# Hawk/FoX decoder step: the second tile's high halves of keys and queries come by an on-chip copy instead of a second load

## The chip, the core and the metric

The kernel runs on one core of one Trainium2 chip. A core has a matrix engine (TensorE, "PE" in the profile, with its weight loads as "PEld"), VectorE (DVE), ScalarE (ACT), GpSimd (POOL) and SyncE (SP), which here does nothing but issue transfers. 16 DMA engines move data between HBM and the on-chip memory, whose tiles have up to 128 partitions (rows). The engines run their own instruction streams in order and wait for one another by semaphores. The metric is the device time of one execution in microseconds.

## The reference, cut to what matters

One step of a small hybrid decoder: a recurrent (RG-LRU) layer, then an attention layer with a forget gate. It runs on a new prompt of 2048 tokens and, beside it, on 8 sequences of 8 new tokens with a paged cache of 4096 past tokens each. The change touches the attention of the prompt alone:

```python
D_MODEL = 1024; SEQ = 2048; N_HEADS = 16; HEAD_DIM = 64
...
def fox_block(q, k, v, cq, ck, q_pos, k_pos):
    s = jnp.einsum('bqhd,bkhd->bhqk', q, k).astype(jnp.float32) * (HEAD_DIM ** -0.5)
    s = s + jnp.swapaxes(cq, 1, 2)[:, :, :, None] - jnp.swapaxes(ck, 1, 2)[:, :, None, :]
    mask = k_pos[None, :] <= q_pos[:, None]
    s = jnp.where(mask[None, None], s, -jnp.inf)
    p = jax.nn.softmax(s, axis=-1)
    return jnp.einsum('bhqk,bkhd->bqhd', p.astype(v.dtype), v)
...
def fox_mixer(x, k, v, cq, ck, q_pos, k_pos, w_in, w_out):
    ...
    return (o * jax.nn.silu(g)) @ w_out
```

`cq` and `ck` are running sums of the log forget values. All data is float32.

## The kernel before, in words

TensorE multiplies in a reduced float32 format, so the kernel keeps float32 accuracy by splitting numbers: x = high + low, and a product is high·high + high·low + low·high. Keys and queries of the prompt are written to HBM in both halves, features first: `kd` and `qd` are [1024 features, 2 halves, 2048 tokens]. In `kd` half 0 is the low part and half 1 the high part; in `qd` it is the other way round.

The execution has three large stages. First come the recurrent layer and the projections, then, from about 1750 us on, the prompt's attention with the decode of the 8 sequences interleaved, and last the output projection. The change lies in the attention.

The attention (`attention`) goes through 16 heads; a head is 40 steps, called ticks. A unit is a head and a block of 512 queries (`qc`, 0 to 3); a tick takes one unit and one block of 128 keys, so unit `qc` has 4(qc+1) ticks. Even heads take the units in the order 0, 1, 2, 3, odd heads in the order 3, 2, 1, 0. In a tick TensorE makes the scores `st` with two matmuls. L1592 multiplies `ka` and `qa`, which have 128 rows each: the low and high rows of the keys against the high and low rows of the queries, that is, both cross products at once. L1593 multiplies `kbt` and `qbt`: 64 rows of high halves, and below them rows for the forget sums, the ones and the row maxima. ACT takes the exponential into a buffer `p` (L1601; six buffers `p`, five `acc`), after every four ticks TensorE multiplies the four `p` with the values `vvt` (L1612), and POOL adds the four `p` into `acc` (recorded at the helper's L108). A `p` is free again when both have read it. At least 8 and up to 18 ticks ahead, another pass (`top`, L1431) multiplies the high halves alone, and DVE takes the row maxima (L1433, L1435).

How the tiles are loaded: `load_keys(h+1)` runs in the first tick of head h and loads 64 rows of high keys into one of two fixed tiles `kbt` (L1399) and three rows of sums (L1400). `load_head(h+1)` runs at tick 16 of head h and loads `ka`, 128 rows with low and high rows interleaved (L1406, two buffers), and the values (L1407). `load_unit` loads the high queries into one of six fixed tiles `qbt` (L1413), `load_low` all 128 rows of `qa` (L1419, four buffers). So the high halves are fetched from HBM twice. All these are issued by SP, except the first ones, before the first tick, which ACT issues; those of head 0 are cut in two by columns.

The order around it: `later` is a list of functions that are called a given number of ticks on. The decode of the cache is a generator that is advanced in proportion (`Side.along`); its page loads `raw` (L1093) are issued by SP in the same queue, and its matmuls (L1148, L1262) are pinned between the attention's. Loads under `paged()` stand behind the last page load. Apart from such pins, the instruction order of each engine is set when the program is built, by a scheduler with a timeline of its own.

Of the kernel before, what the change touches and what calls it, by code (L numbers as in the profile page):

```python
# [12 lines left out]
F32R = mybir.dt.float32r  # L13
# [7 lines left out]
P = 128  # L21
D = 1024
KB = 8
SEQ = 2048
# [4 lines left out]
HD = 64  # L29
# [29 lines left out]
OG = 1  # L59
NQ = 6  # L60
AFT = 14


class Turns:
# [17 lines left out]
def f(ap):  # L82

    return ap.bitcast(F32)
# [3 lines left out]
def tile_hawk_fox(  # L88
# [8 lines left out]
    V, A, G, T, S = nc.vector, nc.scalar, nc.gpsimd, nc.tensor, nc.sync  # L97
# [19 lines left out]
    def paged():  # L117

        return tc.issue_after(place["S"]) if "S" in place else ExitStack()
# [49 lines left out]
    def dt_(name, shape):  # L169
        return dram.tile(shape, F32, name=name, tag=name)  # L170
# [9 lines left out]
    kd_d, qd_d = dt_("kd", [D, 2, SEQ]), dt_("qd", [D, 2, SEQ])  # L180
# [41 lines left out]
    def sbuf(es, name, side=None):  # L222
        return es.enter_context(tc.tile_pool(name=name, bufs=1, side=side, reuse_waits="tile"))
# [150 lines left out]
    later = Later()  # L374
# [959 lines left out]
    def attention(es):  # L1334
        pool = sbuf(es, "att")
# [11 lines left out]
        kbs = [pool.tile([P, SEQ], F32R, name="kbt0")]  # L1347
        qbs = [pool.tile([P, 512], F32R, name=f"qbt{i}") for i in range(NQ)]
        maskb = pool.tile([P, 512], F32, name="maskb")
        kbs.append(pool.tile([P, SEQ], F32R, name="kbt1"))  # L1350
        for i in range(NQ):
            if i % 3 == 0 and i < 6:
                kb = kbs[i // 3]
# [30 lines left out]
        heads, qas, mxs, oTs_, sgt = {}, {}, {}, {}, {}  # L1384
# [4 lines left out]
        def halves(h):  # L1389
            return ((0, half), (half, SEQ)) if h == 0 else ((0, SEQ),)  # L1390


        queue = [A]

        def load_keys(h):
            kb = kbs[h % 2]
            loaded.add(h)
            for lo, hi in halves(h):
                queue[0].dma_start(f(kb[0:64, lo:hi]), kd_d[h * HD:(h + 1) * HD, 1, lo:hi])  # L1399
                queue[0].dma_start(f(kb[64:67, lo:hi]), nc_d[h, :, lo:hi])  # L1400

        def load_head(h):
            hr = slice(h * HD, (h + 1) * HD)
            ka = pool.tile([P, SEQ], F32R, name="ka", tag="ka", bufs=2)
            for lo, hi in halves(h):
                queue[0].dma_start(f(ka[:, lo:hi]), kd_d[h * HD:(h + 1) * HD, :, lo:hi].rearrange("d x t -> (d x) t"))  # L1406
            queue[0].dma_start(vvs[h % 2][:, :, :], v_d[:, hr].rearrange("(k p) d -> p k d", p=P))  # L1407
            heads[h] = ka

        def load_unit(u):  # L1410
            h, qc = units[u]
# [3 lines left out]
        def load_low(u):  # L1415
            if u < len(units):
                h, qc = units[u]
                qa = qas[u] = pool.tile([P, 512], F32R, name="qa", tag="qa", bufs=4)
                queue[0].dma_start(f(qa[:, :]), qd_d[h * HD:(h + 1) * HD, :, qc * 512:(qc + 1) * 512].rearrange("d x t -> (d x) t"))  # L1419

        def top(u, j, ck):

# [69 lines left out]
        def norm(pr, sums, q0, n, oT):  # L1492
# [10 lines left out]
            def gate(qc, sg):  # L1503
# [9 lines left out]
                if n == 4:  # L1513
                    later.after(AFT, store)
                else:
                    store()

            def fetch(qc):
                sg = pool.tile([P, 512], F32, name="sgt", tag="sgt", bufs=2)
                with paged():  # L1520
                    S.dma_start(sg[:, :], sg_d[pr * P:(pr + 1) * P, qc * 512:(qc + 1) * 512])
                later.after(3, lambda: gate(qc, sg))

            for qc in range(q0, q0 + n):
                later.after((3 + 2 * (qc % 2) + (AFT + 7) * (qc // 2) if n == 4 else 2 * (qc - q0)), lambda qc=qc: fetch(qc))

        tasks = [(u, j, ck) for u, (h, qc) in enumerate(units) for j in range(4) for ck in range(qc + 1)]
        nks = [(qc + 1) * 4 for _, qc in units]
        start = [sum(nks[:u]) for u in range(len(units))]
        done = [0, 0, 0]  # L1530

        def advance(tick):
# [6 lines left out]
            while done[0] < min(need, len(tasks)):  # L1539
# [5 lines left out]
                done[0] += 1  # L1545

        load_keys(0)
        tick = 0
        advance(-1)
        load_head(0)  # L1550
        load_low(0)
        load_low(1)
        queue[0] = S
        for _ in range(3):
# [11 lines left out]
                    return psum["dec"].tile([P, 512], F32, name="st", tag="do"[wide[0] // 2 % 2], bufs=1)  # L1566
            return ps3.tile([P, 512], F32, name="st", tag="st", bufs=2)

        lows = [2]

        def loads():
            while lows[0] < len(units):
                v = lows[0]
                if tick < (start[v - 2] if v < 4 else min(max(start[v - 2], start[v - 3] + AFT), start[v] - 3)):
                    break
                with paged():
                    load_low(v)
                lows[0] += 1
            h, k = divmod(tick, 40)
            if k == 16 and h + 1 < H:  # L1580
                with paged():
                    load_head(h + 1)

        for u, (h, qc) in enumerate(units):
            for k in range(nks[u]):
                loads()
                ka, kb = heads[h], kbs[h % 2]
                qa, qb = qas[u], qbs[u % NQ]
                lo = max(0, k - qc * 4) * P
# [41 lines left out]
                if k + sum(nks[u - u % 4:u]) == 0 and h + 1 < H:  # L1631
                    load_keys(h + 1)
# [156 lines left out]
    done = 9  # L1789
# [6 lines left out]
    done = max(done, 41)  # L1796
# [61 lines left out]
    psum["att"] = banks(att, "psa", 6)  # L1858
    cost = sum(4.1 * 0.42 * (512 - max(0, k - qc * 4) * P) + 213 for qc in range(4) for k in range(4 * qc + 4)) * H
    side.along(attention(att), ((16 - FIRST) * TURN - side.spent) / (cost * SPAN))  # L1860
    place.clear()
    side.upto(1e12)
# [38 lines left out]
```

## Time and profile before

| | |
|---|---|
| time, median of 3 runs | 3023.98 us (3017.05 to 3034.43) |
| the profiled execution | 3028.43 us, span 3026.4 us |
| TensorE clock granted, mean | 0.969 |
| HBM traffic | 514.22 MB read, 135.16 MB written |
| DMA queue of SP and ACT | 644.26 MB, 67.4% of 16 engines' span |

An engine's share of the span is the time in which it ran instructions. The "idle before" of a group of instructions names what released it: a wait. The profile's chain follows the last instruction back through what each step waited for. A row of a stretch gives, for a window in microseconds: its length, busy time of PE, PEld, DVE, ACT and POOL with the number of instructions, the granted clock, the mean busy share of the DMA engines and the rate in GB/s. A row of waits gives the total, the number and the longest.

### The profile page before, as it was taken

How to read it: one execution, taken by the hardware profiler on the slowest of the kernel's cores; microseconds unless marked ns; L12 is line 12 of the kernel's file. 1: busy time of each engine (PE TensorE's matmuls, PEld its weight loads, DVE VectorE, ACT ScalarE, POOL GpSimd, SP SyncE). 2: the span in 40 equal slices, each digit the busy share in tenths (PEclk: the TensorE clock that was granted, in tenths of full speed). 3: DMA queues.
4: the chain of work that ended last, by engine and by line, in shares of the span. 5: the costliest groups of instructions: out<-in, count | busy, mean ns of one | idle time of the engine just before them, and what ended most of it. 6: DMA issues, size and time to landing. Idle time of an engine off the chain costs nothing.

```text
span 3026.4 us, 60467 instructions
## 1 busy us (share of the span) xinstructions
PE 2803.4 (93%) x21614; PEld 2252.1 (74%) x21614; DVE 1805.5 (60%) x4012; ACT 1269.9 (42%) x2874; POOL 1084.4 (36%) x1199
## 2 busy tenths in 40 slices
PE   6998999998997999999999699998998999999998
PEld 5997789988887997888889556665665666565687
DVE  6877455425427775676564466656776756655344
ACT  4665342222125665534333234444544444355321
POOL 1653201000002653100000245665575656659422
PEclk9999999999998999999999889999999999999999
DMA  4224546888863226699999968898899888874343
GB/s 123 79 88 133 171 126 191 256 263 281 278 216 91 89 88 194 209 313 338 332 346 326 279 209 243 248 282 255 250 291 287 267 251 265 260 247 122 98 145 110
DMA packets 479103, 653.79 MB, mean 216 GB/s; under 512 B 91291, under 2 KB 277020, under 8 KB 471525
## 3 DMA queue, kind: packets, MB, share of 16 engines
q1 hardware_dynamic: 475174, 644.26, 67.4%
q10 hardware_dynamic: 3340, 3.56, 0.4%
q8 instruction: 171, 2.80, 0.4%
q0 software_dynamic: 288, 2.10, 0.2%
q14 instruction: 130, 1.06, 0.1%
HBM read 514.22 MB, written 135.16 MB: 215 GB/s over the span
## 4 chain that ended last, share of the span: by engine, by line
PE 59%; DMA 16%; DVE 9%; ACT 6%; SPq 5%; issue 3%; POOL 1%; ACTq 0%; DVEq 0%; POOLq 0%
PE ops L1612 7%; PE st L1592 4%; PE y L383 4%; PE y L384 4%; PE y L385 4%; DMA raw<-in_cache_k_dram 4%; PE sx L1431 4%; PE dO L1262 3%; DMA raw<-in_cache_v_dram 3%; PE st L1593 3%; PE dS L1148 3%; PE kv L383 3%; PE kv L385 3%; PE kv L384 3%; SPq L1093 2%
## 5 line engine op out<-in xcount | busy, mean ns | idle before, releaser
L108 POOL TENSOR_TENSOR acc<-acc,p 128x512 f32<-128x512 f32 (+3 forms) x576 | 640.9, 1114 | 347.7 <-PE ops L1612 211.2
L1601 ACT ACTIVATE p<-st 128x512 f32<-128x512 f32 (+3 forms) x576 | 291.3, 525 | 400.1 <-PE st L1593 177.5
L1180 DVE STREAM_TRANSPOSE ktr<-raw 128x1024 f32<-128x1024 f32 x256 | 308.2, 1226 | 125.1 <-DMA raw<-in_cache_k_dram 116.5
L1433 DVE TENSOR_REDUCE mxs<-sx 128x1 f32<-128x512 f32 x384 | 255.0, 681 | 141.0 <-PE sx L1431 139.6
L383 PE MATMUL kv<-wh,xh 128*128 128x256 f32 (+3 forms) x1088 | 310.0, 288 | 6.4 <-ACT wh L427 4.7
L384 PE MATMUL kv<-wl,xh 128*128 128x256 f32 (+3 forms) x1088 | 309.3, 287 | 5.7 <-DVE wl L428 5.7
L385 PE MATMUL kv<-wh,xl 128*128 128x256 f32 (+3 forms) x1088 | 309.6, 286 | 2.7 <-DMA xl<-xld 2.7
L1592 PE MATMUL st<-qa,ka 128*128 128x512 f32 (+3 forms) x640 | 269.9, 422 | 13.3 <-ACT p L1601 7.5
L1612 PE MATMUL ops<-p,vvt 128*64 128x256 f32 (+1 forms) x2176 | 262.9, 369 | 1.0 <-ACT p L1601 0.7
L1431 PE MATMUL sx<-kbt,qbt 96*128 96x512 f32 (+3 forms) x640 | 229.2, 416 | 29.9 <-DMA qbt<-qd 24.2
L1113 POOL TENSOR_TENSOR qw<-qb,amask 128x128 f32<-128x128 f32 x64 | 29.1, 460 | 618.1 <-PE dS L1148 325.3
L428 DVE SCALAR_TENSOR_TENSOR wl<-wst,gv,wh 128x256 fp32r<-128x256 f32 (+1 forms) x384 | 169.4, 504 | 131.8 <-ACT wh L427 131.5
L427 ACT ACTIVATE wh<-wst,gv 128x256 fp32r<-128x256 f32 (+1 forms) x384 | 164.6, 499 | 190.2 <-DMA wst<-in_w_kv_dram 72.7
L1593 PE MATMUL st<-qbt,kbt 128*128 128x512 f32 (+3 forms) x640 | 236.9, 370 | 0.0
L383 PE MATMUL qg<-xh,wh 128*128 128x512 f32 (+2 forms) x640 | 229.4, 359 | 0.0
L384 PE MATMUL qg<-xl,wh 128*128 128x512 f32 (+2 forms) x640 | 228.2, 357 | 0.0
L385 PE MATMUL qg<-xh,wl 128*128 128x512 f32 (+2 forms) x640 | 227.5, 356 | 0.6 <-DVE wl L428 0.6
L1612 PEld LDWEIGHTS ops<-p,vvt 128*64 128x64 f32 x2176 | 161.5, 141 | 88.2 <-issue 19.8
L383 PEld LDWEIGHTS kv<-wh,xh 128*128 128x128 f32 (+1 forms) x1088 | 203.5, 188 | 13.2 <-ACT wh L427 6.8
L384 PEld LDWEIGHTS kv<-wl,xh 128*128 128x128 f32 (+1 forms) x1088 | 203.2, 188 | 10.1 <-DVE wl L428 6.9
L385 PEld LDWEIGHTS kv<-wh,xl 128*128 128x128 f32 (+1 forms) x1088 | 204.8, 188 | 7.0 <-issue 3.7
L1592 PEld LDWEIGHTS st<-qa,ka 128*128 128x128 f32 x640 | 123.7, 193 | 112.8 <-issue 54.4
(297 smaller groups left out, 6356.3 us busy)
## 6 DMA issues: line engine op xcount, KB each, us to landing
raw<-in_cache_k_dram SPq DMA_DIRECT2D x512, 256.0 KB
raw<-in_cache_v_dram SPq DMA_DIRECT2D x512, 256.0 KB
wst<-in_w_kv_dram SPq DMA_DIRECT2D x48, 512.0 KB
wst<-in_b_w_in_dram SPq DMA_DIRECT2D x48, 512.0 KB
xt<-in_x_prompt_dram SPq DMA_DIRECT2D x32, 512.0 KB
wst<-in_a_w_in_dram SPq DMA_DIRECT2D x64, 256.0 KB
out_dram<-kf SPq DMA_DIRECT2D x128, 128.0 KB
sc<-cd SPq DMA_DIRECT2D x16, 1024.0 KB
```

The lines of the kernel that those rows point to most:

```text
L108: eng.tensor_tensor(out, a, b, op=op)
L383: T.matmul(ps, lh(k), rh(k), start=(k == 0), stop=False)
L384: T.matmul(ps, lh(k), rl(k), start=False, stop=False)
L385: T.matmul(ps, ll(k), rh(k), start=False, stop=(k == nk - 1))
L428: V.scalar_tensor_tensor(wl[:, k, :], st[:, k, :], gk, f(wh[:, k, :]), op0=ALU.mult, op1=ALU.subtract)
L1180: behind("V", V.transpose(t.kts[pp][:, n], raw[:, :, pp * 256:(pp + 1) * 256]).ins)
L1431: T.matmul(ps[:, :w], qb[0:96, j * P:(j + 1) * P], kb[0:96, ck * 512:ck * 512 + w], start=True, stop=True)
L1433: place["V"] = V.reduce_max(mx[:, j, ck:ck + 1], ps[:, :w], axis=AX.X).ins
L1592: place["T"] = T.matmul(ps[:, lo:], ka[:, ks], qa[:, lo:], start=True, stop=False).ins
L1593: T.matmul(ps[:, lo:], kb[:, ks], qb[:, lo:], start=False, stop=(k < qc * 4))
L1601: pair.append((k, lo, p, A.activation(p[:, lo:], ps[:, lo:], AF.Exp)))
L1612: return T.matmul(ops[r * HD:(r + 1) * HD, a0 * P:], vvs[h % 2][:, k, :], p[:, :].rearrange("p (a r c) -> p a r c", a=2, r=2)[:, a0:, r, : ...
```

## The change

The high rows of keys and queries are loaded once and copied on the chip to where they are needed a second time. `ka` and `qa` are no longer interleaved: the query's high rows and the key's low rows lie in partitions 0 to 63, the others in 64 to 127.

Keys: `load_high(h)` loads the high rows into the upper half of `ka`, now in the first tick of the head before; nine ticks later (`CAME`) POOL copies them in four pieces of 64x512 into `kbt`. At tick 16 only the low rows and the values are loaded. For head 0 `kbt` is still loaded from HBM. Queries: `load_low` loads only the low rows, and ACT copies the high rows from `qbt` to `qa`, 64x512, four ticks before the unit begins.

```diff
+CAME = 9
...
         def load_keys(h):
             kb = kbs[h % 2]
             loaded.add(h)
+            if h:
+                load_high(h)
+                later.after(CAME, lambda: high(h))
             for lo, hi in halves(h):
-                queue[0].dma_start(f(kb[0:64, lo:hi]), kd_d[h * HD:(h + 1) * HD, 1, lo:hi])
+                if not h:
+                    queue[0].dma_start(f(kb[0:64, lo:hi]), kd_d[:HD, 1, lo:hi])
                 queue[0].dma_start(f(kb[64:67, lo:hi]), nc_d[h, :, lo:hi])
+
+        def high(h):
+
+            for lo in range(0, SEQ, 512):
+                G.tensor_copy(kbs[h % 2][0:HD, lo:lo + 512], heads[h][HD:P, lo:lo + 512])
+
+        def load_high(h):
+
+            ka = heads[h] = pool.tile([P, SEQ], F32R, name="ka", tag="ka", bufs=2)
+            for lo, hi in halves(h):
+                queue[0].dma_start(f(ka[HD:P, lo:hi]), kd_d[h * HD:(h + 1) * HD, 1, lo:hi])
 
         def load_head(h):
             hr = slice(h * HD, (h + 1) * HD)
-            ka = pool.tile([P, SEQ], F32R, name="ka", tag="ka", bufs=2)
+            if not h:
+                load_high(h)
             for lo, hi in halves(h):
-                queue[0].dma_start(f(ka[:, lo:hi]), kd_d[h * HD:(h + 1) * HD, :, lo:hi].rearrange("d x t -> (d x) t"))
+                queue[0].dma_start(f(heads[h][0:HD, lo:hi]), kd_d[hr, 0, lo:hi])
             queue[0].dma_start(vvs[h % 2][:, :, :], v_d[:, hr].rearrange("(k p) d -> p k d", p=P))
-            heads[h] = ka
...
         def load_low(u):
...
-                queue[0].dma_start(f(qa[:, :]), qd_d[h * HD:(h + 1) * HD, :, qc * 512:(qc + 1) * 512].rearrange("d x t -> (d x) t"))
+                queue[0].dma_start(f(qa[HD:P, :]), qd_d[h * HD:(h + 1) * HD, 1, qc * 512:(qc + 1) * 512])
+
+        def high_q(u):
+
+            assert u < done[1]
+            A.copy(qas[u][0:HD, :], qbs[u % NQ][0:HD, :])
...
-        lows = [2]
+        lows, highs = [2], [0]
 
         def loads():
...
+            while highs[0] < lows[0] and tick >= start[highs[0]] - 4:
+                high_q(highs[0])
+                highs[0] += 1
```

## The prediction

> **What bounds the kernel now.** I read the page first (busy shares, DMA queues, the chain that ended last), then the stage that the change touches by windows, then the waits of that stage.
>
> ```profile
> span 3026.4 us, 60467 instructions
> PE 2803.4 (93%) x21614; PEld 2252.1 (74%) x21614; DVE 1805.5 (60%) x4012; ACT 1269.9 (42%) x2874; POOL 1084.4 (36%) x1199
> PE 59%; DMA 16%; DVE 9%; ACT 6%; SPq 5%; issue 3%; POOL 1%; ACTq 0%; DVEq 0%; POOLq 0%
> L1592 PE MATMUL st<-qa,ka x640: 222/403/797, 1749.2 to 2823.9; 128*128 128x512 f32 x160
> core 0: us, PE busy (x) PEld busy (x) DVE busy (x) ACT busy (x) POOL busy (x), PEclk, DMA share, GB/s
> 1800.00:2700.00 900.00, 846.08 (x7720) 540.37 (x7720) 587.35 (x1252) 409.88 (x1017) 561.91 (x535) 0.97 0.85 264
> ```
>
> The page says TensorE: 93% of the span, 59% of the chain. The prompt's attention is 640 score steps ("ticks") from 1749.2 to 2823.9 us, 1.68 us each. In 900 us of it TensorE works 846.08, so 54 us is all that any relief could free there, while the DMA engines are 85% taken, ACT 46% (409.88 of 900) and POOL 62%. The change takes bytes from the DMA engines and gives work to ACT and POOL, so what counts is who makes TensorE wait. The waits from 1756 to 2825 us (in all, times, longest):
>
> ```profile
> PE dO L1262 <- DMA raw<-in_cache_v_dram: 19.4, 13, 3.1
> PE rp L1505 <- DMA r<-rs: 11.5, 6, 4.2
> PE st L1592 <- ACT p L1601: 7.5, 20, 0.8
> PEld st L1592 <- ACT p L1601: 37.6, 87, 1.7
> ACT p L1601 <- POOL acc L108: 38.1, 34, 3.5
> ```
>
> TensorE waits 19.4 us for value pages of the cache (`raw`), which share the DMA engines with the loads that shrink. Before a score matmul its weight load waits for ACT's exponential at 87 of 640 ticks, and ACT in turn waits 38.1 us for POOL's additions, because these return the buffers `p`. No row of that list, in this window, has TensorE waiting for `ka` or `qa`.
>
> **The change, part by part.**
>
> *Bytes.* Issues of the same window, KB each:
>
> ```profile
> DMA packets 157990, 261.15 MB, mean 244 GB/s; under 512 B 48796, under 2 KB 51363, under 8 KB 152825
> ka<-kd SPq DMA_DIRECT2D x15, 1024.0 KB
> kbt<-kd SPq DMA_DIRECT2D x14, 512.0 KB
> qa<-qd SPq DMA_DIRECT2D x60, 256.0 KB
> ```
>
> For 15 heads (all but the first) 1024 + 512 KB become 512 + 512, and for 64 units `qa` goes from 256 to 128 KB: 7.9 + 8.4 = 16.3 MB less, 6% of 261.15. The number of issues on SP stays (two key loads a head, two query loads a unit); only the high half of `ka` moves, from tick 16 of the head before to its start. There it stands on SP where the `kbt` load stood, and waits, as that did, for the last score matmul of the head that is over; the page loads queued behind it wait no longer than before: 0.
>
> But what remains are loads of 64 partitions, and bytes aren't engine time. Two issues and the stretches behind them in which their packets ran:
>
> ```profile
> 2308.19 0.45 SPq L1399 DMA_DIRECT2D kbt<-kd  x1
> 2309.40:2311.60 2.20, 2.20 (x18) 1.46 (x18) 0.12 (x1) 0.74 (x2) 0.89 (x1) 1.00 1.02 227
> 2323.70 0.33 SPq L1406 DMA_DIRECT2D ka<-kd  x1
> 2327.20:2329.40 2.20, 2.20 (x18) 1.35 (x16) 2.20 (x4) 1.04 (x3) 2.04 (x3) 1.00 1.03 405
> ```
>
> Behind the 64-partition load all engines are taken (1.02) at 227 GB/s; behind the 128-partition load (1.03) at 405. So 0.524 MB on half the partitions costs 0.524/0.227 = 2.31 us, and 1.049 MB on all of them 1.049/0.405 = 2.59 us. A head's keys cost 2.31 + 2.59 = 4.90 us before and 2 x 2.31 = 4.62 after: 0.28 us saved, 4 us over 15 heads, instead of 15 x 0.524/0.405 = 19 us. If the 2 KB rows of the queries behave alike (no row shows them alone) they save nothing; at full rate 8.4/0.405 = 21 us. Of the engine time, what TensorE feels is at most its 19.4 us on value pages. I take -1 us, nearest to the key rows; bounds 0 and -19.
>
> The Trainium skill, "SBUF — State Buffer", section "Door 1", says the same as a rule: partitions 0 to 63 reach only 8 of 16 DMA ports, so half a tile moves at half the rate, and two half-tile transfers don't add up. Its 196 GB/s for 64 partitions would make the half load 2.7 us (an estimate from that page), two of them 5.4, so by it the key traffic would even grow by 0.5 us a head; the rows above give 2.31 us, and by them it doesn't.
>
> *Start.* For head 0 both halves of `ka` are now separate, in two column halves: four issues on ACT's queue for two, ahead of `vvt` and `qa`. The chain there:
>
> ```profile
> 1738.71 0.44 ACTq L1406
> 1739.67 9.45 DMA qa<-qd
> 1749.16 0.80 PE st L1592
> ```
>
> The first score matmul starts when `qa` has landed. Two issues more are 0.9 us; two half loads at 2.31 us for one full at 2.59 are 2.0 us ahead of it in the engines. Bounds 0 and +3; I take +2. The copies of `qa` for units 0 and 1 run while it lands.
>
> *ACT.* 64 copies of 64x512 from `qbt` to `qa`, four ticks before each unit. Nearest rows:
>
> ```profile
> L1484 ACT COPY cs<-tot 128x512 f32<-128x512 f32 x15 | 8.8, 586 | 0.8 <-PE tot L1481 0.7
> L1466 ACT COPY oT<-ops 64x256 f32<-64x256 f32 x126 | 46.2, 367 | 76.6 <-PE ops L1612 75.8
> ```
>
> At 0.59 us (same row length; 0.37 is for half of it) that is 64 x 0.59 = 38 us on an engine with more than half its time free. The copy's inputs are long there, so it waits for nothing; queued behind it is the next exponential, for which TensorE waits. TensorE's weight load stood for ACT at 87 of 640 ticks, 14%: there a delay passes on whole. 0.14 x 38 = 5 us. Bounds 0 (all in ACT's gaps) and 38.
>
> *POOL.* 15 x 4 copies of 64x512 from the upper to the lower partitions, nine ticks into the head before:
>
> ```profile
> L1357 POOL MEMSET qbt<- 64x512 f32 x6 | 3.0, 535 | 0.1
> L103 POOL TENSOR_SCALAR uh<-uc 128x384 fp32r<-128x384 f32 x32 | 23.2, 726 | 57.5 <-DVE uc L594 49.7 <-PE g L385 4.9 <-ACT up L705 2.9
> L103 POOL TENSOR_SCALAR co<-cs 128x1024 f32<-128x1024 f32 x4 | 4.3, 1078 | 38.4 <-DMA qsd<-qf 18.8 <-PE qg L385 14.4 <-DVE cs L339 5.2
> L108 POOL TENSOR_TENSOR acc<-acc,p 128x512 f32<-128x512 f32 x384 | 496.2, 1292 | 238.3 <-PE ops L1612 153.3 <-ACT p L1601 54.6 <-ACT sc L1217 5.8
> ```
>
> On the line between the two TENSOR_SCALAR rows 512 elements take 726 + 128 x (1078 - 726)/640 = 796 ns; a fill takes 535, an addition with two inputs 1292. I take 0.8: 3.2 us a head, 48 us in all (bounds 32 and 78). The Trainium skill, "GPSIMD Engine Reference", section 3.1, gives 1.03 cycles an element to a body with one input, at 1.2 GHz 0.44 us for 512 (an estimate, without dispatch); by it POOL's part would be 26 us, and no row here shows it.
>
> What it costs depends on POOL's place in the head. At nine ticks of an odd head, and all through head 14:
>
> ```profile
> 2382.11 0.47 SPq L1399 DMA_DIRECT2D kbt<-kd  x1
> DMA packets 1054, 2.29 MB, mean 283 GB/s; under 512 B 136, under 2 KB 136, under 8 KB 988
> 2383.05 10.80 POOL L108 TENSOR_TENSOR acc<-acc,p 128x512 f32<-128x512 f32 x8 [2.85 <-PE ops L1612]
> 2391.00 0.50 PE L1592 MATMUL st<-qa,ka 128*128 128x512 f32 x1
> 2394.11 4.00 POOL L108 TENSOR_TENSOR acc<-acc,p 128x512 f32<-128x512 f32 x3 [0.26 <-ACT p L1601]
> 2720.50:2773.00 52.50, 50.15 (x294) 31.01 (x294) 35.32 (x55) 31.99 (x65) 49.09 (x40) 1.00 0.57 159
> ```
>
> Head 9 begins with a wide unit, and POOL adds without a break up to 2393.85, past tick 9 at 2391.00; 3.2 us of copies push the next additions back, the buffers `p` come free later, ACT and then TensorE wait. Six buffers, four additions to a product group, leave about two ticks of play, so I count 0.5 us for each of the seven odd heads, 3.5 us. Even heads begin with short units and smaller additions: 0. In head 14 the decode has ended and POOL is busy 49.09 of 52.50 us, so all 3.2 us count. Sum +6; bounds 0 and 48.
> The copies also wait for their load. The slowest issue is head 9's, 2382.11. In the stretch 2382.1 to 2390.2 (second row) 1054 - 988 = 66 packets of 8 KB and more ran, 64 of them the keys': landed as tick 9 starts, and POOL is busy 3 us longer. I count 0.
>
> *Sum.* -1 + 2 + 5 + 6 = +12 us. Against the profiled execution, 3028.43 us for a span of 3026.4, that is 3040; it stood 4.4 us above the median of the three runs, 3023.98, so for the median 3036.
>
> **The rivals.**
> *Relief* (the other side). If queries at half the partitions run at full rate and keys queue better, the value pages come in time: 3024 - 19 (value pages) - 3 (a quarter of the 11.5 us on `r`, small transfers in the same queue) = 3002 with the copies hidden. It decides when 64-partition 2 KB packets take no longer than 128-partition ones. Against it: the 227 GB/s. 0.15.
> *Nothing*: engine time as before and both copies in gaps, 3024 + 2 = 3026. For it: ACT 46%, POOL 62% busy. 0.12.
> *POOL waits for the keys.* POOL works in order. If SP, behind its page loads, issues some 5 us later, POOL stands 5 us in each of 15 heads, two of them covered by the buffers: 45 us, 3069. It decides at a landing 2 us after tick 9; head 9 has about that to spare. 0.15.
> *ACT copies fall before exponentials that are due*, all 38 us pass: 3024 + 2 + 38 = 3064. Against it: 14% of the ticks. 0.08.
>
> **How the numbers follow.** The forecast has 0.5, with its own range 3022 to 3052 (POOL 0 to 20, ACT 2 to 10). 0.5%, 15 us, is about what a measurement of this kernel tells from no change: faster is below 3009, slower above 3039. Faster: relief, 0.15, with 0.01 from the forecast's edge. Same: 0.12 of nothing and 0.29 of the forecast, 0.41. Slower: 0.15 + 0.08 + 0.20 of the forecast, 0.43. The range 3004 to 3064 leaves out about a tenth at each end: most of relief, and POOL's wait.
>
> **What would show it.** Bytes 16 MB down with the DMA share of 1800 to 2700 us within 0.02 of 0.85; behind the upper-half load again about 227 GB/s; ACT copies near 0.59 us and POOL copies near 0.8; ACT's wait for POOL's additions up from 38.1 us, above all in head 14; TensorE's first score some 2 us later. I am wrong if the DMA share falls by 0.04 or more and the 19.4 us shrink (relief), or if POOL shows waits for a `ka` load.

## The result, and the profile after

The changed kernel takes 3067.16 us (median of 4 runs, 3066.44 to 3073.8) against 3024.32 for the kernel before in the same session (4 runs, 3017.05 to 3034.43): ratio 1.0127, 95% interval 1.0098 to 1.0156. That is 43 us slower. The forecast was 3036 with a range up to 3064: slower was the likelier side, by little (0.43 against 0.41 for no change), and the size was missed by 31 us, 3 us beyond the range.

The page of the changed kernel, profiled execution 3073.8 us:

```profile
span 3072.1 us, 60693 instructions
PE 2823.7 (92%) x21614; PEld 2261.3 (74%) x21614; DVE 1803.5 (59%) x4012; ACT 1300.7 (42%) x2938; POOL 1114.0 (36%) x1259
PE 47%; DMA 17%; DVE 8%; SPq 5%; ACT 4%; issue 3%; POOL 1%; ACTq 0%; DVEq 0%; POOLq 0%
HBM read 497.97 MB, written 135.16 MB: 206 GB/s over the span
```

The bytes fell by 514.22 - 497.97 = 16.25 MB, as worked out. ACT got 64 instructions and 31 us of work, POOL 60 and 30 us. TensorE's 47% of the final chain can't be set against the 59% before: followed back, the chain of this profile ends at 465 us (its shares add up to 85%), that of before reaches the start.

The next two fences are stretches of the attention, of the kernel before and of the changed one. The first row runs from the first score to the end of the last one, the next two are heads 0 to 6 and 7 to 13, the fourth heads 14 and 15. Columns: length, then busy time (and instructions) of TensorE's matmuls, weight loads, DVE, ACT, POOL, then granted clock, DMA share, GB/s.

```profile
1749.16:2824.24 1075.08, 1012.07 (x8866) 645.10 (x8866) 684.64 (x1437) 501.92 (x1220) 684.40 (x640) 0.97 0.79 244
1749.16:2242.28 493.12, 466.33 (x4251) 298.38 (x4251) 326.55 (x672) 216.43 (x532) 297.27 (x287) 0.95 0.82 253
2242.28:2720.45 478.17, 448.54 (x4039) 286.65 (x4039) 304.71 (x671) 224.17 (x560) 292.81 (x276) 0.98 0.85 263
2720.45:2824.24 103.79, 97.20 (x581) 60.07 (x579) 53.38 (x99) 61.32 (x129) 94.32 (x79) 1.00 0.39 112
```

```profile
1749.86:2869.66 1119.80, 1031.81 (x8865) 654.15 (x8865) 681.69 (x1434) 528.94 (x1280) 713.97 (x697) 0.95 0.75 220
1749.86:2251.32 501.46, 469.10 (x4252) 300.33 (x4252) 324.57 (x672) 228.56 (x559) 307.89 (x308) 0.95 0.81 237
2251.32:2753.77 502.45, 458.16 (x4036) 290.66 (x4035) 303.05 (x665) 236.68 (x586) 310.55 (x307) 0.95 0.80 234
2753.77:2869.66 115.89, 104.55 (x584) 63.16 (x582) 54.07 (x100) 63.69 (x136) 95.53 (x84) 0.93 0.32 88
```

Nearly all of the loss lies here: the attention grew by 44.7 us, the span by 45.7. TensorE stands (length less busy) 63.0 us before and 88.0 after: 25 us more. The other 20 us are the same matmuls at a lower granted clock (0.95 for 0.97); how much of that may belong to the single execution, the control below shows. The DMA engines' time in heads 0 to 13, length times share, is 493.12 x 0.82 + 478.17 x 0.85 = 811 us before and 501.46 x 0.81 + 502.45 x 0.80 = 808 after: some 14 MB fewer there by the rates, and the same engine time.

A half load (head 8's keys, from SP's timeline) and the stretch behind it, with columns as above, show why:

```profile
2251.36 0.45 SPq L1416 DMA_DIRECT2D ka<-kd  x1
```

```profile
2252.60:2254.80 2.20, 2.20 (x18) 1.41 (x14) 2.20 (x3) 1.06 (x4) 2.09 (x4) 1.00 1.00 226
```

226 GB/s with all engines taken, for 227 in the kernel before. Next waits of the changed kernel in the attention (in all, times, longest), from the views of TensorE, ACT and POOL:

```profile
PE rp L1526 <- DMA r<-rs: 15.5, 6, 4.2
PE st L1616 <- ACT p L1625: 12.6, 29, 2.3
PE mps L1469 <- DVE mrow L1465: 12.1, 6, 4.5
PE dO L1263 <- DMA raw<-in_cache_v_dram: 11.6, 6, 3.9
PE sx L1452 <- DVE mxs L1456: 9.4, 5, 5.1
...
PE sx L1452 <- DVE mxs L1454: 5.1, 12, 1.2
```

```profile
ACT p L1625 <- POOL acc L109: 37.5, 37, 2.8
ACT qa L1440 <- PE st L1616: 21.6, 16, 5.3
```

```profile
POOL acc L109 <- PE ops L1636: 203.8, 44, 21.5
...
POOL kbt L1410 <- DMA ka<-kd: 50.3, 13, 9.3
```

TensorE's wait for value pages fell from 19.4 to 11.6, ACT's for POOL stayed (38.1, now 37.5). What grew is spread: DVE's maxima (the three rows with `mxs` and `mrow` make 26.6 us, 10.0 before), the small `r` (15.5 for 11.5), the exponentials (12.6 for 7.5). New are two waits of the copies, which no row of before has: POOL stands 50.3 us for the keys' half load, ACT 21.6 us for a `qa` buffer. The copies' own prices, by groups:

```profile
L1410 POOL CAST kbt<-ka 64x512 fp32r<-64x512 f32 x60 | 34.4, 614 | 63.0 <-DMA ka<-kd 62.8
L1440 ACT CAST qa<-qbt 64x512 fp32r<-64x512 f32 x64 | 39.2, 618 | 57.2 <-DMA ka<-kd 34.2 <-PE st L1616 21.6
```

### The profile page after: what moved, and what is told of

It is laid out like the page before. It is cut to its first block, busy times and chain, and to the rows that moved or that the text cites. A ratio compares the mean times of both kernels' runs of the same rounds, so it can differ in the third digit from the quotient of the medians.

```text
span 3072.1 us, 60693 instructions
## 1 busy us (share of the span) xinstructions
PE 2823.7 (92%) x21614; PEld 2261.3 (74%) x21614; DVE 1803.5 (59%) x4012; ACT 1300.7 (42%) x2938; POOL 1114.0 (36%) x1259
## 3 DMA queue, kind: packets, MB, share of 16 engines
HBM read 497.97 MB, written 135.16 MB: 206 GB/s over the span
## 4 chain that ended last, share of the span: by engine, by line
PE 47%; DMA 17%; DVE 8%; SPq 5%; ACT 4%; issue 3%; POOL 1%; ACTq 0%; DVEq 0%; POOLq 0%
PE ops L1636 7%; DMA raw<-in_cache_k_dram 4%; PE st L1616 4%; PE sx L1452 3%; PE dS L1149 3%; PE y L385 3%; PE y L384 3%; PE y L386 3%; PE st L1617 3%; DMA raw<-in_cache_v_dram 3%; PE dO L1263 3%; PE kv L384 2%; PE kv L385 2%; PE kv L386 2%; SPq L1094 2%
## 5 line engine op out<-in xcount | busy, mean ns | idle before, releaser
L1616 PE MATMUL st<-qa,ka 128*128 128x512 f32 (+3 forms) x640 | 273.0, 427 | 23.1 <-ACT p L1625 12.6
```

What stands on the lines that cost most here:

```text
L1616: place["T"] = T.matmul(ps[:, lo:], ka[:, ks], qa[:, lo:], start=True, stop=False).ins
```

## The experiments

All of them in one table; the sections follow the order in which they were thought of. "Stands" is TensorE's length less busy time between first and last score, "heads 14, 15" the length of those two, both from one profiled execution, which can lie off the median of its kernel (queries only by 19 us), so a few us between two entries say little. A ratio is to the kernel before as timed on the same chip beside it (3024 to 3028 us), and losses in us are against that.

| kernel | loads | copies | us | ratio (95%) | stands | heads 14, 15 |
|---|---|---|---|---|---|---|
| before | 2 whole, 1 half | none | 3024.32 | 1 | 63.0 | 103.8 |
| changed | halves, once | both | 3067.16 | 1.0127 (1.0098 to 1.0156) | 88.0 | 115.9 |
| keys only | queries twice | POOL | 3083.09 | 1.0177 (1.0137 to 1.0218) | 104.4 | 115.3 |
| queries only | keys three halves | ACT | 3062.6 | 1.0108 (1.0074 to 1.0143) | 99.3 | 109.7 |
| three halves | all three halves | none | 3087.26 | 1.0195 (1.0163 to 1.0228) | 107.9 | 107.9 |
| no copies | halves, once | none | 3051.49 | 1.0078 (1.0053 to 1.0102) | 79.1 | 106.4 |
| keys pinned | halves, once | both | 3095.44 | 1.0212 (1.0163 to 1.0261) | 118.4 | 112.2 |
| queries pinned | halves, once | both | 3060.78 | 1.0106 (1.0084 to 1.0127) | 91.1 | 113.8 |
| both pinned | halves, once | both | 3086.06 | 1.0209 (1.0178 to 1.0239) | 106.5 | 111.1 |
| control | as before, two swapped | none | 3032.84 | 1.0016 (1.0002 to 1.0031) | 64.7 | 104.2 |
| changed, lead 16 | halves, once | both | 3062.19 | 1.0108 (1.0066 to 1.0149) | 91.0 | 117.6 |
| before, lead 16 | as before | none | 3031.56 | 1.0008 (0.9985 to 1.0031) | 72.1 | 101.2 |
| copies over loads | as before | both | 3090.31 | 1.0204 (1.0167 to 1.0241) | 108.3 | 114.6 |
| copies in place | as before | both | 3055.6 | 1.0114 (1.0084 to 1.0143) | 88.2 | 117.3 |

### One half of the change alone, and neither

The first theory was that the two new waits make the loss: POOL stands for the keys, ACT for a `qa` buffer. The rival was the half loads. So first each copy alone, with the other tile's second load put back as half loads, and then all halves loaded with no copy.

Keys only (ACT's copies out, both query halves loaded):

```diff
+                queue[0].dma_start(f(qa[0:HD, :]), qd_d[h * HD:(h + 1) * HD, 0, qc * 512:(qc + 1) * 512])
                 queue[0].dma_start(f(qa[HD:P, :]), qd_d[h * HD:(h + 1) * HD, 1, qc * 512:(qc + 1) * 512])
...
-            while highs[0] < lows[0] and tick >= start[highs[0]] - 4:
-                high_q(highs[0])
-                highs[0] += 1
```

> Keys as in the changed kernel (POOL copies the high rows into kbt); the queries' high rows are loaded twice from HBM again, as two 64-row loads into qa, and ACT copies nothing. Theory (POOL standing 50.3 us for the key load, and ACT standing 21.6 us for a qa buffer, put there by the order in which the build places the copies, make the 43 us): about 70% of it stays, 3050 to 3058. Rival 1 (the copies' own time, 34 us on POOL and 39 on ACT, whatever they wait for): half of it, 3045. Rival 2 (64-row loads make the transfers late, the copies cost nothing): 3067 or more, since there is one more half load a unit.

Queries only (POOL's copies out, `kbt` loaded from HBM again, both halves of `ka` at tick 16):

```diff
-            if h:
-                load_high(h)
-                later.after(CAME, lambda: high(h))
             for lo, hi in halves(h):
-                if not h:
-                    queue[0].dma_start(f(kb[0:64, lo:hi]), kd_d[:HD, 1, lo:hi])
+                queue[0].dma_start(f(kb[0:64, lo:hi]), kd_d[h * HD:(h + 1) * HD, 1, lo:hi])
...
-            if not h:
-                load_high(h)
+            load_high(h)
```

> Queries as in the changed kernel (ACT copies the high rows into qa); the keys' high rows are loaded twice from HBM, 64 rows into kbt and 64 into ka, and POOL copies nothing. Theory: the ACT part alone, 3035 to 3042. Rival 1: half of the loss, 3046. Rival 2: 3067 or more.

Three halves (both of these edits together: the changed layout, no copy, every high half loaded twice):

> No copies; keys and queries get three 64-row loads each (kbt and both halves of ka; qbt and both halves of qa) where the kernel before has one of 64 and one of 128 rows. By the rates of the trace before this adds 3 x 2.31 - 4.90 = 2.0 us of DMA engine time a head, 30 us, and up to 0.6 us a unit, 38 us. Theory (the DMA engines aren't what binds): 3024 to 3036. Rival 2 (half loads make transfers late): 3060 or more, and waits for value pages well over 19.4 us.

No copies (the loads of the changed kernel, and neither copy; the rows that the copies would fill keep zeros, in fixed tiles, so the scores lack the high halves; TensorE's work is the same):

```diff
+        V.memset(f(kbs[1][0:HD, :]), 0.0)
+        qfix = [pool.tile([P, 512], F32R, name=f"qa{i}") for i in range(4)]
+        for t in qfix:
+            V.memset(f(t[0:HD, :]), 0.0)
...
-                later.after(CAME, lambda: high(h))
...
-                qa = qas[u] = pool.tile([P, 512], F32R, name="qa", tag="qa", bufs=4)
+                qa = qas[u] = qfix[u % 4]
...
-            while highs[0] < lows[0] and tick >= start[highs[0]] - 4:
-                high_q(highs[0])
-                highs[0] += 1
```

> Leaves out both copies: the loads are those of the changed kernel, but kbt (from the second head on) and the lower half of qa keep zeros, so the scores lack the high halves. TensorE's work is the same. Theory: the whole loss goes, and the 16 MB less bring almost nothing: 3015 to 3027. Rival 2: 3060 or more. A DMA relief hidden by the copies would show as 3005 or less.

The whole attention of three halves, then TensorE's longest wait in it, then the whole attention and heads 14 and 15 of the kernel without copies:

```profile
1749.83:2887.47 1137.64, 1029.79 (x8866) 652.26 (x8866) 685.31 (x1437) 502.17 (x1219) 682.85 (x640) 0.95 0.81 231
```

```profile
PE dO L1263 <- DMA raw<-in_cache_v_dram: 39.2, 14, 5.7
```

```profile
1748.76:2847.62 1098.86, 1019.76 (x8864) 647.55 (x8864) 683.02 (x1434) 501.12 (x1216) 684.69 (x641) 0.96 0.78 224
2741.19:2847.62 106.43, 100.23 (x584) 61.70 (x582) 53.15 (x100) 61.20 (x131) 94.96 (x80) 0.97 0.36 96
```

All four miss what the first theory gave. Two things follow. A half load more costs engine time and TensorE feels it: three halves take 1137.64 x 0.81 = 921 us of the engines where the kernel without copies takes 1098.86 x 0.78 = 857 (each from its first row), TensorE's wait for value pages goes to 39.2 us, and the time from 3051 to 3087. So about 36 us for 64 us of engine time (the shares are rounded to 0.01, which leaves some 10 us of play in the 64). And the loads of the changed kernel alone, with no copy and within 1% of the engine time of before (1075.08 x 0.79 = 849), lose 25 us (0.53 to 1.02%). The prediction had put them at -1. The rest of the change's loss, from 1.0078 to 1.0127 or some 15 us, is what the copies cost on top of these loads. The two separate halves of the change, keys only and queries only, are mixtures, since each carries the extra loads of the other tile; neither beats the whole change by more than the intervals.

### Taking the copies' waits away

If POOL's 50.3 us make the loss, it must go when the copies run later, after their load has landed. Keys pinned: the copies may not be placed ahead of the last addition that stands before them in the program.

```diff
         def high(h):
-            for lo in range(0, SEQ, 512):
-                G.tensor_copy(kbs[h % 2][0:HD, lo:lo + 512], heads[h][HD:P, lo:lo + 512])
+            with tc.issue_after(place["G"]):
+                for lo in range(0, SEQ, 512):
+                    G.tensor_copy(kbs[h % 2][0:HD, lo:lo + 512], heads[h][HD:P, lo:lo + 512])
...
-                            tt(a_l(), acc[:, lo:], acc[:, lo:], p[:, lo:], ALU.add)
+                            place["G"] = G.tensor_tensor(acc[:, lo:], acc[:, lo:], p[:, lo:], op=ALU.add).ins
```

> The changed kernel, with POOL's key copies pinned in POOL's order behind the additions traced up to the ninth tick, so that the build can't place them earlier. Theory: POOL no longer stands for the key load (50.3 us before, now under 10), two thirds of the loss go: 3035 to 3045. Rival 1 (the copies' own time): no change, 3062 to 3072. Rival 3 (any new order costs this much): anywhere, with POOL's wait gone and the time not lower.

Queries pinned: the same for ACT's copies, behind the last exponential.

```diff
-            A.copy(qas[u][0:HD, :], qbs[u % NQ][0:HD, :])
+            with tc.issue_after(place["A"]) if "A" in place else ExitStack():
+                A.copy(qas[u][0:HD, :], qbs[u % NQ][0:HD, :])
...
                 pair.append((k, lo, p, A.activation(p[:, lo:], ps[:, lo:], AF.Exp)))
+                place["A"] = pair[-1][3].ins
```

> The changed kernel, with ACT's query copies pinned in ACT's order behind the last exponential traced, four ticks before the unit. Theory: ACT no longer stands for a qa buffer (21.6 us before, now under 3), a quarter to a third of the loss goes: 3050 to 3058. Rival 1: no change, 3062 to 3072.

Both pinned:

> Both pins. Theory: both waits gone, what stays is the predicted +12 us or less: 3022 to 3036. Rival 1: no change, 3062 to 3072. Rival 3: anywhere, unrelated to the two waits.

The copies' group on POOL with the keys pinned, and TensorE's and POOL's largest waits there:

```profile
L1411 POOL CAST kbt<-ka 64x512 fp32r<-64x512 f32 x60 | 35.4, 632 | 1.0
```

```profile
PE mps L1470 <- DVE mrow L1466: 27.4, 10, 6.2
PE rp L1527 <- DMA r<-rs: 27.2, 6, 8.3
```

```profile
POOL acc L1645 <- PE ops L1637: 252.0, 44, 31.1
```

POOL's stand for the load is gone (1.0 us of idle time ahead of 60 copies, for 63.0), and the kernel is 28 us slower than the change, not faster. The theory finds no support. POOL has time to stand: it waits 203.8 us for TensorE's products in the changed kernel, and what it no longer stands for the load it stands for TensorE (252.0 here). TensorE now waits for DVE's row of maxima 27.4 us for 12.1; that the later copies squeeze the next head's top pass, which reads `kbt`, would explain it, but no run shows it apart. The pin also moved the order on TensorE (next but one section), so a share of POOL's wait in the 43 us isn't excluded. Pinning ACT's copies takes ACT's wait for `qa` away and moves the time by less than the intervals (1.0106 for 1.0127).

### A control

The kernel before, with the three rows of sums loaded ahead of the keys: nothing but two issues swapped, which is enough for the build to make another order of instructions.

```diff
-                queue[0].dma_start(f(kb[0:64, lo:hi]), kd_d[h * HD:(h + 1) * HD, 1, lo:hi])
                 queue[0].dma_start(f(kb[64:67, lo:hi]), nc_d[h, :, lo:hi])
+                queue[0].dma_start(f(kb[0:64, lo:hi]), kd_d[h * HD:(h + 1) * HD, 1, lo:hi])
```

> The kernel before with one pair of issues swapped (the 24 KB load of the sums ahead of the 512 KB key load): no work is added or taken away, only the build's order is disturbed. Theory: within 10 us of 3024. Rival 3 (the order alone explains the loss): 20 us or more off, either way.

```profile
1741.93:2832.24 1090.31, 1025.59 (x8866) 650.23 (x8866) 687.91 (x1437) 502.39 (x1220) 683.93 (x640) 0.95 0.78 240
```

It takes 0.16% more, and TensorE stands 64.7 us, as before (63.0). But its matmuls took 1025.59 us at a clock of 0.95. So 13.5 us of longer matmuls, for the changed kernel's 20, appear in a profile whose kernel is about 5 us slower by its ratio: the busy time of one execution says little here, the standing time more.

### Does the order on TensorE make the loss?

The build gives each engine its order by a timeline of its own. Counted against the scores, the top pass (`sx`) stands 2.3 ticks earlier in the changed kernel than before, and 4.4 ticks earlier with the keys pinned, the slowest of those with the same loads. The next theory was that this shift makes the loss. `LEAD`, the ticks by which the program runs the top pass ahead, moves it back.

```diff
-LEAD = 18
+LEAD = 16
```

The changed kernel with this edit (shift against the kernel before -0.1 ticks):

> The changed kernel with the lead of the planner over the scores set to 16 ticks for 18, so that the top pass stands in the built order where it stood before the change (-0.1 ticks for -2.3). By the theory of the order: the part of the loss that hangs on the order comes back, 3030 to 3050, and the waits for mrow (12.1) and r (15.5) fall towards 6 and 11. Rival, the loads and copies themselves cost the time: 3060 to 3075 as the change.

The kernel before with this edit (shift +1.2 ticks):

> Control: the kernel before with the same lead of 16. In its built order the top pass moves 1.2 ticks later than before. By the theory of the order it is equal or a little slower: 3018 to 3035. If it gains as much as the changed kernel gains by the lead of 16, then the lead itself is worth that, and says nothing of the change.

The mean position came back and the time didn't: 3062.19, within the interval of the change; TensorE stands 91.0 us for 88.0. The kernel before doesn't mind the lead (1.0008). So the mean position of the top pass isn't the cause; that the pinned kernels got slower with it doesn't carry over. And the control and this kernel, both with an order other than before and nothing added, lose 0.16 and 0.08%: a new order needn't cost.

### The copies without the half loads

Both copies added to the kernel before, all of its loads kept. First over the loaded rows:

```diff
             loaded.add(h)
+            if h:
+                later.after(9, lambda: again(kb))
...
+        def again(kb):
+            for lo in range(0, SEQ, 512):
+                G.tensor_copy(kb[0:HD, lo:lo + 512], kb[0:HD, lo:lo + 512])
...
+            while highs[0] < lows[0] and tick >= start[highs[0]] - 4:
+                A.copy(qas[highs[0]][0:HD, :], qbs[highs[0] % NQ][0:HD, :])
+                highs[0] += 1
```

> The kernel before with all its loads as they were, and both kinds of copies added over tiles that are loaded anyway: ACT copies qbt over the loaded upper half of qa four ticks before its unit, POOL copies the keys in kbt onto themselves nine ticks in. The values stay the same. By the theory of TensorE's order: in the built order the top pass stands 1.3 ticks earlier against the scores than before, so some 20 to 35 us are lost, 3045 to 3060, and TensorE's waits for mrow and r grow. Rival, the half loads make the loss and the copies none: within 8 us of the kernel before. Rival, loads and copies add up (after +43, loads without copies +25): +18, 3035 to 3048.

The values don't stay the same: the rows of `qa` alternate high and low in the kernel before, so this copy puts high rows on low ones and changes the scores. Its time can be read, but not for the question: ACT waits for each `qa` load before it may write over it.

```profile
ACT qa L1586 <- DMA qa<-qd: 115.8, 44, 5.5
```

So this kernel measures a wait of its own: 62 us. The second form reads and writes one tile, `qbt`, which landed long before:

```diff
-                A.copy(qas[highs[0]][0:HD, :], qbs[highs[0] % NQ][0:HD, :])
+                A.copy(qbs[highs[0] % NQ][0:HD, :], qbs[highs[0] % NQ][0:HD, :])
```

> The kernel before with all its loads as they were, and copies of the same number, shape and place in the program that read and write one tile, so that ACT's wait for no load: ACT copies the query's high half in qbt onto itself four ticks before its unit, POOL the keys' high half in kbt onto itself nine ticks in. Theory that loads and copies add up (loads without copies +24 us, change +43): +15 to +20 us, 3040 to 3046, of which 8 to 12 in heads 14 and 15 (103.8 us before, 111 to 118 in every kernel with POOL's copies). Rival, the copies cost nothing without the half loads: within 6 us, heads 14 and 15 at 101 to 106. Rival, the copies alone make the whole loss: +35 or more. Theory of the order (the top pass built 1.3 ticks earlier): +20 to +35.

The whole attention and heads 14 and 15 of it, and the waits of ACT and POOL at the copies:

```profile
1744.19:2850.03 1105.84, 1017.60 (x8866) 647.44 (x8866) 684.41 (x1437) 530.56 (x1283) 712.88 (x696) 0.96 0.77 237
2732.78:2850.03 117.25, 102.34 (x581) 61.71 (x579) 51.03 (x96) 63.41 (x134) 94.82 (x83) 0.94 0.36 103
```

```profile
ACT qbt L1586 <- PE sx L1437: 32.5, 18, 5.2
```

```profile
POOL kbt L1406 <- DMA kbt<-kd: 42.9, 12, 7.2
```

29 us by the medians, 1.0114 (1.0084 to 1.0143): two thirds of the loss or more with the loads of the kernel before, and TensorE stands 88.2 us, as long as in the changed kernel. Together with the kernel without copies (1.0078) this says that either part alone is enough to lose more than half of it, and that they don't add up: 0.78 + 1.14% is 1.92%, and the change loses 1.27%. The sum that I expected here, 3040 to 3046, was too low. Two reserves: copying in place has ACT wait 32.5 us for the top pass, which still reads `qbt`, where the change has ACT wait 21.6 us for a `qa` buffer; the two aren't the same wait. And POOL waits here for the load of `kbt` (last row) nearly as long as for `ka` in the change, 42.9 us for 50.3, so this kernel doesn't show the copies without that wait.

### Where the copies cost: head 14

One place can be read closely. In heads 14 and 15 the eight kernels with POOL's copies take 111.1 to 117.6 us, the six without 101.2 to 109.7: no overlap, whatever their loads. The difference lies in head 14 (52.6 us before, 64.8 after), where POOL copies the last head's keys and the output projection's weights (`wst`) are already being fetched and split. The timeline of the changed kernel there (start, length, engine, what, idle before and releaser):

```profile
2758.02 6.06 SPq L1435 DMA_DIRECT2D qa<-qd  x1
...
2764.38 0.50 PE L1616 MATMUL st<-qa,ka 128*128 128x512 f32 x1
...
2764.74 1.97 DVE L1454 TENSOR_REDUCE mxs<-sx 128x1 f32<-128x512 f32 x3
2764.81 7.60 SPq L483 DMA_DIRECT2D wst<-in_b_w_out_dram  x3
...
2765.48 1.04 PE L1452 MATMUL sx<-kbt,qbt 96*128 96x512 f32 x2 [0.31 <-DVE mxs L1454]
...
2766.76 1.04 PE L1452 MATMUL sx<-kbt,qbt 96*128 96x512 f32 x2 [0.25 <-DVE mxs L1454]
...
2768.05 1.10 PE L1452 MATMUL sx<-kbt,qbt 96*128 96x512 f32 x2 [0.25 <-DVE mxs L1454]
...
2769.70 1.05 ACT L102 CAST woh<-wst 128x1024 fp32r<-128x1024 f32 x1 [4.99 <-DMA wst<-in_b_w_out_dram]
2770.78 0.60 ACT L1625 ACTIVATE p<-st 128x512 f32<-128x512 f32 x1
...
2771.43 0.69 PE L1616 MATMUL st<-qa,ka 128*128 128x384 f32 x1 [2.28 <-ACT p L1625]
```

Between two scores TensorE's order holds six top-pass matmuls in a row. Each pair waits for DVE's maximum of an earlier one, so they go at DVE's pace, 0.64 us apiece, and end at 2769.15. What ends the tick comes later: ACT stands 4.99 us for the weights `wst`, whose issue on SP began only at 2764.81, behind one for `qa` that held the queue 6.06 us; the next exponential stands behind the weights in ACT's order and starts at 2770.78, and the next score waits 2.28 us for it. The same count for the kernel before and the changed one, top-pass matmuls alone, in the ticks about the end of the head's short units:

```profile
2730.80:2735.70 4.90, 0.81 (x2) 0.39 (x2) 1.00 1.10 264
```

```profile
2764.38:2771.43 7.05, 2.96 (x6) 1.12 (x6) 0.86 0.88 225
```

Two in three ticks of 4.90 us before, six in one tick of 7.05 after. In the kernel before, SP is held for a `qa` buffer as well, but ACT's order is another:

```profile
2722.51 0.38 SPq L482 DMA_DIRECT2D wst<-in_b_w_out_dram  x1
...
2725.74 7.63 SPq L1419 DMA_DIRECT2D qa<-qd  x1
...
2734.01 1.05 SPq L482 DMA_DIRECT2D wst<-in_b_w_out_dram  x2
```

```profile
2730.76 1.05 ACT L101 CAST woh<-wst 128x1024 fp32r<-128x1024 f32 x1 [2.50 <-DMA wst<-in_b_w_out_dram]
...
2740.50 1.05 ACT L101 CAST woh<-wst 128x1024 fp32r<-128x1024 f32 x1
```

ACT's 2.50 us are for the fourth load of these weights, issued before the hold (2722.51). The fifth, issued behind it (2734.01), is cast at 2740.50 without a wait; in ACT's order that cast stands behind 15 of the head's 40 exponentials. In the changed kernel the fifth cast stands behind 5, and ACT reaches it before the weights have come. Counted in all traces, it stands behind 5 to 7 exponentials in the six kernels with POOL's copies unpinned, behind 11 or 12 where the keys are pinned, and behind 11 to 15 in the six without.

Every kernel with POOL's copies has a tick with 4 to 7 top-pass matmuls that is 6.3 to 13.3 us long in head 14 (at tick 8 or 9, at tick 18 where the copies are pinned later); the kernels without them have no tick of three or more that is longer than 4.5 us. Such rows aren't the whole of it: the longest tick of this head in the changed kernel, tick 18, takes 8.1 us with one top-pass matmul, and no copies and three halves have ticks of 6.9 and 5.5 us with none. The order is fixed when the program is built, so the copies don't only delay what stands behind them: with them in it the build fills TensorE's and ACT's order otherwise.

Heads 0 to 13 remain. There the changed kernel is 33 us longer, 20 of them TensorE standing (56.4 to 76.7 us by the rows above), and no single wait or head carries it: the waits for DVE, ACT and `r` are each some us longer, and the heads lie from 6.5 us shorter to 10.5 us longer. The control's profile is 15 us longer there too, but in busy time: TensorE stands 57.8 us in it. It stands 73 us both with the copies in place and with the half loads alone, at an engine time within 1% of before; but the kernel before with lead 16, which loses nothing, stands 66. So a loss goes with each of the two, and by what path in these heads is open.

## Why the prediction was right or wrong

**Bytes: the engine time right, its effect wrong.** 16.25 MB less (16.3 worked out), 226 GB/s behind a half load (227), engine time unchanged. The DMA share of 1800 to 2700 us fell by 0.03 (to 0.82), past the 0.02 I allowed, since the stretch of work got longer, not because the engines had less to do. The 0.5 us a head by which the keys were to grow at the lower rate sets two loads at 2.7 us against a sum in which the half load of the kernel before still counts 2.31; at 2.7 for that one too it is 0.1. But I took equal engine time as an effect of -1 us, and the loads without copies lose 25 us. This is the first step that failed, and it was outside its bounds of 0 and -19: loads of the same engine time in another shape and place weren't free, and I had excluded a loss without a reason. What made them cost stays open.

**Start.** First score 1749.16 to 1749.86: +0.7 for +2.

**ACT and POOL: prices right, reach wrong.** 618 ns a copy on ACT (0.59 taken), 614 on POOL (0.8 taken, bound 32 us in all; it was 34.4). I counted +5 and +6 by asking what stands behind the copy in an order that stays as it was (the POOL sum, 3.5 + 3.2, is 6.7 and not 6). Copies alone, with their waits, cost 29 us; on top of the half loads it was some 15, near the 11 counted, but that is no proof of the count, since the order moved under it. Taking the order as fixed is the second step that failed. Head 14 was the right place, at 3.2 us; heads 14 and 15 lost 12. The sign that I named for it, ACT's wait for POOL up from 38.1, didn't come (37.5): in head 14 the copies act through the order on TensorE and ACT, and ACT waits for the buffers `p` no longer than before.

**"I count 0" for the copies' load.** POOL does stand 50.3 us for it, 13 times. The build put the copies ahead of tick 9 (the first of a head's four ran before it in 14 of 15 heads, mostly at ticks 1 to 8), and my landing time was set against a tick that nothing enforced.

**The rivals.** "POOL waits for the keys" has its sign in the profile and its price, 3069, is 2 us from the result. It isn't borne out as the cause: with the wait taken away the kernel gets slower, though the pin that did it moved the order as well. A right time and a matching wait were not enough to prove the mechanism. "Relief" fell as argued: half loads of keys run at 226 GB/s, and the equal engine time leaves little room for queries at full rate; the wait for value pages did fall, by 7.8 us, while the time rose. "Nothing" fell too. "ACT copies pass fully" (3064) wasn't separated: the pinned queries moved the time less than can be told, and they left the copies on ACT.

**The direction.** That the time rose was forecast, but narrowly and from +2, +5 and +6, while 25 of the 43 us come from the loads that stood at -1. The right side was in large part luck.

## What to carry to other kernels

An operation added to a tuned, in-order program is not only its duration: it can change the order that the build makes, and copies of 34 and 39 us on two engines that were idle a third and half of the time cost 29 us here. So compare the built orders, and not only the waits. Before believing a wait, take it away: a wait on an engine that has slack (POOL here, 203.8 us of waiting for TensorE) may only change its name. And a load on half the partitions saved bytes here, not engine time; compare loads by the time that they take the engines, and leave room for a loss even where that is equal.

## What the runs showed of the hardware

The same count of matmuls took 1012.07 us in one kernel's attention at a granted clock of 0.97 and 1025.59 at 0.95 in a kernel only 0.16% slower, so the busy time of single executions differs by about 1% here. Fetching the high halves a second time, as half loads, cost 64 us of engine time over the attention and 36 us of the kernel: at a share of 0.78 to 0.81 about half of the added engine time was felt, though TensorE's waits for value pages had been only 19.4 us before.
